# A decoder block on one Trainium2 core: a third merge-gate pair in the block scheme, fewer score matmuls for compressed keys, half buffers for attention weights

## The chip, the core and the metric

The kernel runs on one core of a Trainium2 chip. The core has a matmul engine (PE, with its weight loads PEld), a vector engine (DVE), an activation engine (ACT), a general engine (POOL) and a queue engine (SP) that issues most transfers; POOL issues some too. The engines run their own instruction lists in order and wait for each other through semaphores. PE writes to PSUM, eight banks of 128 x 512 float32; all else lies in SBUF or in the memory of the chip.

The metric is the time of one execution on the device in microseconds. Three runs of the kernel before took 1549.4, 1545.86 and 1548.6 us; their median is 1548.6.

## The reference

One layer of a hybrid decoder block, batch 1, 1024 positions, width 1024, all in float32. What is computed, cut to its core:

```python
h = rms_norm(x, norm1_g)
zq, zkv, zg, zr, zm = split(h @ w_in)              # 512, 768, 24, 2048, 2048 columns
y_nsa = nsa_attention(zq, zkv, zg, ...)            # 8 heads of 64 in 2 groups, 3 branches
y_ret = retention(zr)                              # 4 heads of 128
u = stack([y_nsa @ w_branch[0], y_ret @ w_branch[1]])
gates = sigmoid(zm)                                # 2 x 1024 columns: the merge gates
x = x + sum(gates * u) @ w_out
h = rms_norm(x, norm2_g)
x = x + (silu(h @ ffn_w_gate) * (h @ ffn_w_up)) @ ffn_w_down      # 2816 wide
```

The attention has three branches with one softmax each: compressed keys (63 blocks, from a small network over overlapping blocks of 32 positions), eight selected blocks of 64 keys (chosen by the compressed branch's weights), and a window of 512 keys. Scores are q.k/8 minus a slope per head times the distance, and masked:

```python
sc = einsum('btgrd,bngd->bgrtn', qg, kc) * scale - slopes * c_dist
p_cmp = masked_softmax(sc, c_dist >= 0)
```

## The kernel before

**Numbers.** A float32 product is made of three fast products: each operand is split into a high and a low part (ACT copies the high part, DVE subtracts to get the low one; a "fill"), and hi.hi, hi.lo and lo.hi are accumulated in one PSUM bank. So one product of 128 output rows, 512 columns and a depth of 512 is 12 matmuls with 512 moving columns.

**Block scheme.** Large products are done as 2 x 2 blocks with seven block products in place of eight (Strassen-Winograd); sums of blocks are made on DVE. For the input projection the scheme runs over pairs of 128-column units (`r_pairs`, L474): `gseq` (L1139) lists the block products as (product, pair), `g_loads` (L1154) fetches the two weight tiles of each pair, `g_ops` and `g_wsums` make operands, `g_main` issues the matmuls, `g_store` and the functions beside it add up and store the results. Before the change the pairs are two of merge gates (columns 7 and 6 of `m_units`) and eight of retention. The first two pairs do all seven products here; for the retention pairs, products 1 and 2 are done earlier by `gates_first` (L912) and fetched back from memory.

**Merge gates done directly.** The other six columns of merge gates, 12 units of 128 columns, are done by `merge_gates` (L1533) with `half_mm`: two halves of 24 matmuls for each unit. They have the lowest priority in the attention stage, so the scheduler puts them wherever PE has nothing else to do. In the rows these are matmuls from H, the normalised input, against `wh`.

**Attention.** 16 units `u` = (group, block of 128 queries); `us` lists them. For each, `cmp_all` (L1569) does the compressed branch: eight matmuls write four heads' scores, for each head one with the high part of the compressed keys (`kc[:, g, 0]`) and one with the low part; then DVE's `ttr` adds the mask table `Mc`, scales and finds the maximum in one instruction; ACT takes the exponential. `produce_all` (L1644) does the scores of the two other branches in blocks of two heads, into buffers P of two rows of 1024; `p_exp` and `p_scale` turn them into weights; `consume_all` (L1706) transposes them on PE four tiles at a time into a PSUM bank psT, splits them into pT (ACT, then DVE) and multiplies them with the values into psO. Query tiles `qt` come from memory through POOL into two buffers (`q_loads`); a buffer is free again when the scores that use it are done (`q_drop`). `P_ring` has three P buffers, given out in turn.

**Retention** shares the stage with attention. When the last unit's output y is stored, `y_loads` fetches it back, and the branch projections, the output projection and the FFN follow.

**The order.** The work is written as generators that yield operations. `Sched` (L161) keeps a time for each engine and each tile by a table of costs and always issues the operation that could start first; ties go by priority. `SLACK` (L50) is how much earlier than needed an operand has to be ready before an operation counts as startable: 600 ns for PE. Each cost has a duration and a latency until others see the result. All this happens when the program is built; on the chip the order is fixed.

## Time and profile before

| what | value |
|---|---|
| median of three runs | 1548.6 us |
| profiled execution | 1546.82 us |
| its span, first to last instruction | 1545.1 us |
| mean granted clock of PE | 0.997 |
| 0 to 120 us: PE busy | 115.37 us |
| 120 to 330 us (projections): PE busy | 209.12 us |
| 330 to 780 us (attention, retention, merge gates): PE busy | 442.08 us |
| 780 to 930 us (merge, output projection): PE busy | 148.56 us |
| 930 to 1320 us (FFN up): PE busy | 389.65 us |
| 1320 us to the end (FFN down): PE busy | 219.63 us |

In the rows of the profile, `out<-in` are the program's tile names; psS, psT, psO and psF are groups of PSUM banks (three, two, one and two). `xN` counts the instructions of a row. In a timeline row the first number is the start in us, the second the time to the last end of the group; consecutive matmuls overlap, so the time that one costs is read from start to start. A bracket gives the idle time of the engine before the row and what ended it. PE busy times include matmuls' overlapping ends.

### The profile page before, as it was taken

What the parts mean: (1) busy time and instruction counts of PE and PEld (TensorE: products, weight loads), DVE (VectorE), ACT (ScalarE), POOL (GpSimd) and SP (SyncE); (2) the same over time, 40 slices, a digit from 0 to 9 for tenths busy, and PEclk for the clock granted to TensorE, in tenths of its full rate; (3) what the DMA queues carried; (4) which work ended last, traced back from release to release, by engine and by line L of the source; (5) the groups of instructions that cost most, each with busy time, mean ns of one, the idle gap of its engine ahead of it and who ended that gap; (6) DMA issues with size and microseconds to landing.
All of it is one profiled execution on the core that took longest, in us unless ns stands there. A gap on an engine that the chain in (4) does not pass through costs nothing.

```text
span 1545.1 us, 22782 instructions
## 1 busy us (share of the span) xinstructions
PE 1524.4 (99%) x7959; PEld 1300.2 (84%) x7959; DVE 1111.2 (72%) x2364; ACT 754.7 (49%) x1527; POOL 262.5 (17%) x367
## 2 busy tenths in 40 slices
PE   9999999999999999999999999999999999999998
PEld 8887888888899988888888887888888888888887
DVE  7677967738798867798667467777667767676674
ACT  6355542218767777777415335433334333444442
POOL 3001400012232221221000001232332333000000
PEclk9999999999999999999999999999999999999999
DMA  7975975463432444244493224244544544597421
GB/s 219 257 236 168 299 233 161 144 201 92 141 104 78 126 132 130 83 142 153 150 341 129 104 82 123 96 136 141 186 140 145 184 145 144 201 381 255 163 69 55
DMA packets 210421, 249.79 MB, mean 162 GB/s; under 512 B 22657, under 2 KB 138369, under 8 KB 209410
## 3 DMA queue, kind: packets, MB, share of 16 engines
q1 hardware_dynamic: 197186, 206.39, 41.4%
q0 software_dynamic: 13120, 41.95, 8.7%
q8 instruction: 62, 1.02, 0.3%
q14 instruction: 53, 0.43, 0.1%
HBM read 171.73 MB, written 78.66 MB: 162 GB/s over the span
## 4 chain that ended last, share of the span: by engine, by line
PE 88%; DVE 6%; DMA 2%; ACT 1%; issue 1%; POOL 1%; SPq 1%; DVEq 0%; POOLq 0%; ACTq 0%
PE psS L316 31%; PE psF L316 27%; PE psO L316 14%; PE psT L316 11%; PE psT L321 5%; DVE P L1567 1%; DMA qt<-q_scr 1%; DMA yraw<-y_scr 1%; PE psF L321 1%; SPq L370 1%; PE psO L321 1%; DVE pT L346 0%; DVE H L346 0%; DVE P L351 0%; ACT P L336 0%
## 5 line engine op out<-in xcount | busy, mean ns | idle before, releaser
L316 PE MATMUL psF<-H,wh 128*128 128x512 f32 x876 | 223.9, 394 | 0.0
L316 PEld LDWEIGHTS psF<-H,wh 128*128 128x128 f32 x876 | 160.5, 188 | 29.3 <-ACT aw L336 0.4
L316 PE MATMUL psS<-H,wh 128*128 128x512 f32 (+1 forms) x678 | 167.0, 378 | 0.5 <-ACT H L336 0.5
L316 PEld LDWEIGHTS psS<-H,wh 128*128 128x128 f32 x678 | 115.9, 189 | 18.3 <-ACT H L336 1.0
L336 ACT ACTIVATE P<-P,pm 128x640 f32<-128x640 f32 (+7 forms) x128 | 94.1, 736 | 45.4 <-DVE pm L1567 43.5
L346 DVE TENSOR_TENSOR pT<-psT,pT 128x512 fp32r<-128x512 f32 (+1 forms) x152 | 91.6, 615 | 27.9 <-ACT pT L336 27.6
L316 PE MATMUL psS<-kT,qt 128*128 128x384 f32 (+3 forms) x384 | 102.3, 346 | 0.0
L316 PE MATMUL psO<-pT,vv 128*128 128x256 f32 x528 | 92.0, 291 | 2.5 <-DVE pT L346 2.5
L336 ACT ACTIVATE pT<-psT 128x512 fp32r<-128x512 f32 (+1 forms) x152 | 77.2, 534 | 34.2 <-PE psT L321 33.6
L316 PEld LDWEIGHTS psO<-pT,vv 128*128 128x128 f32 x528 | 78.7, 189 | 11.0 <-DVE pT L346 4.8
L321 PE MATMUL psT<-ident,P 128*128 128x128 f32 x528 | 76.9, 273 | 0.7 <-DVE pT L346 0.6
L346 DVE TENSOR_TENSOR wh<-wraw,wh 128x512 fp32r<-128x512 f32 (+1 forms) x66 | 60.0, 913 | 20.2 <-ACT wh L336 20.1
L336 ACT ACTIVATE wh<-wraw 128x512 fp32r<-128x512 f32 (+1 forms) x67 | 53.6, 805 | 42.2 <-PE psT L316 17.8
L316 PEld LDWEIGHTS psS<-kT,qt 128*128 128x128 f32 x384 | 63.9, 190 | 6.5 <-DVE pm L1567 0.8
L321 PEld LDWEIGHTS psT<-ident,P 128*128 128x128 f32 x528 | 61.2, 140 | 4.8 <-issue 1.2
L316 PE MATMUL psS<-wo,H 128*128 128x512 f32 x216 | 58.6, 392 | 0.0
L336 ACT ACTIVATE P<-P,pc 128x640 f32<-128x640 f32 (+7 forms) x68 | 46.9, 710 | 11.9 <-DVE pc L346 11.4
L316 PE MATMUL psS<-op 128*128 128x512 f32 (+1 forms) x240 | 51.1, 354 | 0.0
L369 POOL DMA_DIRECT2D qt<-q_scr x16 | 12.2, 764 | 218.9 <-PE psF L316 130.9
L316 PE MATMUL psF<-sh,op 128*128 128x512 f32 x192 | 46.7, 391 | 0.8 <-DVE sh L346 0.6
L316 PEld LDWEIGHTS psS<-wo,H 128*128 128x128 f32 x216 | 40.2, 188 | 8.1
L316 PEld LDWEIGHTS psS<-op 128*128 128x128 f32 x240 | 41.0, 189 | 6.9
(588 smaller groups left out, 3628.7 us busy)
## 6 DMA issues: line engine op xcount, KB each, us to landing
wraw<-in_w_in_dram SPq DMA_DIRECT2D x30, 512.0 KB, 4.3
f_scr<-fs SPq DMA_DIRECT2D x22, 512.0 KB, 3.6
row<-in_ffn_w_down_dram POOLq DMA_DIRECT2D x22, 512.0 KB, 4.6
t_scr<-row POOLq DMA_DIRECT2D x22, 512.0 KB, 3.6
qt<-q_scr POOLq DMA_DIRECT2D x16, 512.0 KB, 4.5
st<-t_scr SPq DMA_DIRECT2D x31, 256.0 KB, 4.2
z_scr<-zs SPq DMA_DIRECT2D x24, 256.0 KB, 2.0
wraw<-in_ffn_w_gate_dram SPq DMA_DIRECT2D x12, 512.0 KB, 3.9
```

Source lines behind the costliest of these rows:

```text
L316: lambda: pe.matmul(o, l, r, start=start, stop=stop, skip_group_check=True))
L321: return Op("pe", 109, 100, [o], [i], lambda: pe.transpose(o, i, ident))
L336: return Op("act", c, 150, outs, ins, lambda: act.activation(o, i, func, scale=scale, **kw))
L346: return vop(o, [a, b], lambda: (eng or dve).tensor_tensor(o, a, b, op), eng)
L369: r = Op("gp", 1040, lat, [o], [i], lambda: gp.dma_start(o, i)) if eng is gp else \
L370: Op("sp", 50, lat, [o], [i], lambda: sp.dma_start(o, i))
L1567: lambda: dve.tensor_tensor_reduce(o, a, b, -sc, init, ALU.add, ALU.min, acc))
```

## The change

- `NZ = 3`: the first three pairs of the block scheme are merge gates (columns 7, 6 and 5). The third pair's products are listed in a sequence of its own in `gseq`, and the places that distinguished pairs 0 and 1 from the others compare with NZ. `merge_gates` does columns 4 to 0: 10 units.
- Compressed scores: the mask table `Mc` becomes an operand of PE (fp32r, made in Mw's space and copied). For each unit one matmul with the identity writes the mask to the first 64 of each head's 128 columns; then one matmul a head multiplies the queries with both parts of the keys at once, 128 columns: the high part's scores are added to the mask, the low part's scores stand beside them. ACT copies the low part's scores to the new tile cB, and `ttr` adds it in the place where it added the mask.
- P buffers: a block of up to 512 keys takes a half buffer. `Parts` gives out six halves by a plan made ahead (`P_plan`); larger blocks take two halves of one buffer.
- The scheduler's table: PE's slack 240 ns in place of 600, the latency of a matmul's result 230 in place of 100, the costs of matmuls and of POOL's operations set anew.

```diff
-SLACK = {"pe": 600.0, "act": 40.0, "dve": 40.0, "gp": 0.0, "sp": 0.0}
+SLACK = {"pe": 240.0, "act": 40.0, "dve": 40.0, "gp": 0.0, "sp": 0.0}
...
+class Parts(Ring):
+
+
+    def __init__(self, tiles, plan):
+        self.tiles, self.plan, self.n, self.busy, self.was = tiles, plan, 0, {}, {}
+
+    def units(self):
+        a, w = self.plan[self.n]
+        return range(a, a + w)
+
+    def can(self):
+        return not any(u in self.busy for u in self.units())
+
+    def alloc(self, sched):
+        us = self.units()
+        t = self.tiles[us[0] // 2][:, :, us[0] % 2 * 512:us[0] % 2 * 512 + 512 * len(us)]
...
-        c = max(108.0, n * RATE[0] + 3) if r.dtype == F32R else 4 * max(53.5, n * 0.4167 + 1)
-        return Op("pe", c, 100, [o], [l, r],
+        c = max(111.0, n * 0.4427 + 5 if n < 512 else 227.0) if r.dtype == F32R else 4 * max(53.5, n * 0.4167 + 1)
+        return Op("pe", c, 230, [o], [l, r],
...
-            return Op("gp", 70 + 2.4 * n, 150, [o], ins, fn)
+            return Op("gp", 180 + 2.3 * n, 70, [o], ins, fn)
...
-    r_pairs = [(-1, 7), (-1, 6)] + [(h, i) for h in range(4) for i in (2, 0)]
+    NZ = 3
+    r_pairs = [(-1, 7 - n) for n in range(NZ)] + [(h, i) for h in range(4) for i in (2, 0)]
...
     for f in range(2, GN):
-        gseq += [(6, f), (4, f - 1), (5, f), (3, f - 1), (7, f)]
+        if f < NZ:
+            gseq += [(1, f), (4, f - 1), (2, f), (3, f - 1), (6, f), (5, f), (7, f)]
+        else:
+            gseq += [(6, f), (4, f - 1), (5, f), (3, f - 1), (7, f)]
...
-        for c in range(5, -1, -1):
+        for c in range(7 - NZ, -1, -1):
...
-    P_ring = sb_ring(ap_, [128, 2, T], F32, "P", 3)
+    P_plan, at = [], 0
+    for (g_, i_), br_, pr_ in blocks:
+        w = 2 if i_ >= 4 else 1
+        at += at % 2 if w == 2 else 0
+        P_plan.append((at % 6, w))
+        at += w
+    P_ring = Parts([ap_.tile([128, 2, T], F32, name="P", bufs=3) for _ in range(3)], P_plan)
...
+            sv = s.rearrange("p (r a n) -> p r a n", r=4, a=2)
+            yield mm(sv[:, :, 0, :], identr, Mc[:, None, 56 - 8 * i:120 - 8 * i].to_broadcast([128, 4, 64]), True, False)
             for r in range(4):
-                yield mm(s[:, r * 64:(r + 1) * 64], qt[u][:, 0, r, :], kc[:, g, 0, :], True, False)
-                yield mm(s[:, r * 64:(r + 1) * 64], qt[u][:, 0, r, :], kc[:, g, 1, :], False, True)
+                yield mm(s[:, r * 128:(r + 1) * 128], qt[u][:, 0, r, :], kc[:, g].rearrange("p a n -> p (a n)"), False, r == 3)
             q_drop(u)
+            sB = fresh(ap_, [128, 4, 64], F32, "cB")
+            yield ac(sB, sv[:, :, 1, :])
             for r in range(4):
-                yield ttr(P[:, r, :], s[:, r * 64:(r + 1) * 64], Mc[:, 56 - 8 * i:120 - 8 * i],
-                          2.0 ** -(4 * g + r + 1), 3e38, m[:, r:r + 1])
+                yield ttr(P[:, r, :], sv[:, r, 0, :], sB[:, r, :], 2.0 ** -(4 * g + r + 1), 3e38, m[:, r:r + 1])
```

Over the whole program PE has 7805 instructions before and 7743 after: 12 fewer of 512 columns, 128 matmuls of 64 columns replaced by 64 of 128 and 16 of 256, two fewer of the matmuls that warm PE up at the start. ACT has 16 copies more. The order of all engines is made anew; from the end of the output projection on it is the same on PE but for a few matmuls that change places by one.

What stands on PE in the projection stage, before. The rows are block products of 12 matmuls each, named by their operands (gRS, gSa, gSb and H are blocks of the input and their sums; wh and oq hold weights):

```order
L316 MATMUL psF<-gSb,oq 128x512 x12
L316 MATMUL psS<-gRS,oq 128x512 x12
L316 MATMUL psS<-gRS,wh 128x512 x12
L316 MATMUL psS<-H,wh 128x512 x12
L316 MATMUL psO<-gSa,wh 128x512 x12
L316 MATMUL psF<-gSb,wh 128x512 x12
L316 MATMUL psS<-gRS,oq 128x512 x24
```

The same place on PE after:

```order
L346 MATMUL psF<-gSb,oq 128x512 x12
L346 MATMUL psS<-gRS,oq 128x512 x12
L346 MATMUL psS<-H,wh 128x512 x24
L346 MATMUL psT<-H,wh 128x512 x12
L346 MATMUL psF<-gSb,wh 128x512 x12
L346 MATMUL psS<-gRS,oq 128x512 x12
L346 MATMUL psO<-gSa,oq 128x512 x12
L346 MATMUL psS<-gRS,oq 128x512 x24
```

The third pair's products 1 and 2 (the rows from H into psS and psT) have come in between the second pair's last ones, and its products 6, 5 and 7 follow.

What stands on PE ahead of the compressed scores of the third unit of the second group, before. With buffer numbers: qt_5810 is the query tile of the unit before, qt_6132 the one that is waited for; kT0 and kT1 are keys, kc the compressed keys; rd, re, rS and rc belong to retention. The last use of the tile whose buffer qt_6132 takes stands six rows above the first row shown:

```order
L316 MATMUL psO_6099<-pT_6112,vv1_5863 128x256 x2
L321 MATMUL psT_6148<-ident_78,P_5939 128x128 x2
L316 MATMUL psS_6155<-kT1_5635,qt_5810 128x256 x2
L316 MATMUL psF_6091<-rd_5577,re_6088 128x128
L316 MATMUL psF_6091<-rS_5801,rc_6047 128x128
L316 MATMUL psF_6091<-rd_5577,re_6088 128x128
L316 MATMUL psS_5817<-H_85,wh_5075 128x512 x2
L316 MATMUL psO_6099<-pT_6151,vv1_5863 128x256 x2
L321 MATMUL psT_6187<-ident_78,P_6042 128x128 x2
L316 MATMUL psS_6145<-kc_146,qt_6132 128x64 x8
```

The same place on PE after (qt_5822 is the tile of the unit before, qt_6084 the new one); the last use of the buffer's old tile stands nine rows above the first row shown:

```order
L346 MATMUL psF_6053<-rd_5744,re_6049 128x128
L346 MATMUL psF_6053<-rS_5911,rc_5913 128x128
L346 MATMUL psS_6124<-kT1_5653,qt_5822 128x256 x2
L346 MATMUL psF_6053<-rd_5744,re_6049 128x128
L346 MATMUL psO_6117<-pcT_5692,vc_150 128x512
L351 MATMUL psT_6134<-ident_78,P_3144 128x128 x2
L346 MATMUL psS_6144<-kT0_5821,qt_5822 128x256 x2
L351 MATMUL psT_6136<-ident_78,cPd_5987 128x128 x4
L346 MATMUL psS_5761<-H_85,wh_4924 128x512 x5
L346 MATMUL psS_6174<-kT0_5821,qt_5822 128x256 x2
L346 MATMUL psS_6186<-Mc_154,identr_83 128x4x64
L346 MATMUL psS_6186<-kc_149,qt_6084 128x128 x4
```

More of the unit's own scores (rows with kT0, kT1 and qt_5822) now stand ahead of the next unit's compressed scores, which are a mask matmul and four of 128 columns where there were eight of 64.

What stands on PE at the end of attention, before (psO<-pT,vv are output products, psT<-ident,P transpositions of weights):

```order
L316 MATMUL psF<-H,wh 128x512 x5
L316 MATMUL psO<-pT,vv_6095 128x256 x4
L316 MATMUL psF<-H,wh 128x512 x3
L316 MATMUL psO<-pT,vv_6095 128x256 x4
L316 MATMUL psF<-H,wh 128x512 x45
L316 MATMUL psS<-H,wh 128x512 x36
```

And after:

```order
L346 MATMUL psF<-H,wh 128x512 x5
L346 MATMUL psO<-pT,vv_6102 128x256 x4
L346 MATMUL psF<-H,wh 128x512 x3
L346 MATMUL psO<-pT,vv_6102 128x256 x4
L346 MATMUL psF<-H,wh 128x512 x42
L346 MATMUL psS<-H,wh 128x512 x36
```

Three matmuls fewer stand between the last output product and the first that needs its result (in the psS row).

More of the change, by code (lines that the diff above doesn't have):

```diff
@@ L137, in release @@
         raise ValueError("not live")
+class Parts(Ring):
[9 more added lines that the diff above has]
+        t = self.tiles[us[0] // 2][:, :, us[0] % 2 * 512:us[0] % 2 * 512 + 512 * len(us)]
+        name = key(t)[0]
+        for u in us:
+            for hh in range(2):
+                k = (name, hh * 2 + u % 2)
+                sched.seed[k] = sched.used.get(k, 0.0)
+            self.busy[u] = t
+        self.n += 1
+        return t
+    def release(self, t):
+        for u in [u for u, e in self.busy.items() if e is t]:
+            del self.busy[u]
 class Bag(Ring):
@@ L319, in tr @@
         if i.dtype == F32R:
-            return Op("pe", 56, 100, [o], [i], lambda: pe.transpose(o.bitcast(F32R), i, identr))
-        return Op("pe", 109, 100, [o], [i], lambda: pe.transpose(o, i, ident))
+            return Op("pe", 56, 230, [o], [i], lambda: pe.transpose(o.bitcast(F32R), i, identr))
+        return Op("pe", 109, 230, [o], [i], lambda: pe.transpose(o, i, ident))
     def ac(o, i, scale=1.0, func=AF.Copy, bias=None, accum=None):
@@ L401 @@
         "H": lambda off: off // 1024 % NT,
-        "P": lambda off: off // 1024,
+        "P": lambda off: off // 512,
         "xx": lambda off: off // 1024,
@@ L480 @@
     GN = len(r_pairs)
-    z_units = [pair_unit(f, 0) for f in range(2, GN)]
+    z_units = [pair_unit(f, 0) for f in range(NZ, GN)]
     a_scr = [dram.tile([128, 512], F32, name=f"a_scr{f}") for f in range(GN)]
-    for c, b in ((7, 1), (7, 0), (6, 1), (6, 0)):
+    for c, b in [(7 - n, b) for n in range(NZ) for b in (1, 0)]:
         z_scr[c, b] = dram.tile([128, T], F32, name=f"z_scr{c}_{b}")
-    order = [u for c in range(5, -1, -1) for u in m_units[c][::-1]] + b_units[1] + b_units[0] + o_units[:4] + o_units[6:]
+    order = [u for c in range(7 - NZ, -1, -1) for u in m_units[c][::-1]] + b_units[1] + b_units[0] + o_units[:4] + o_units[6:]
     def half_mm(hl, half, o, k0=0, nk=8, mov=None, step=1):
@@ L504 @@
     gate = att.tile([128, NT, NH, 3], F32, name="gate")
-    Mc = att.tile([128, 128], F32, name="Mc")[:, 0:120]
+    Mc = att.tile([128, 128], F32R, name="Mc")[:, 0:120]
     few = att.tile([128, 8, 8], F32, name="few")
@@ L833, in tables @@
         fl.add("rt")
-        yield g(Mc, lambda: gp.iota(Mc, pattern=[[16, 120]], base=-865, channel_multiplier=-1, **kw))
-        yield sel(Mc, [[-16, 120]], NEG, 865, 1)
+        M0c = Mw[:, 0:120]
+        yield g(M0c, lambda: gp.iota(M0c, pattern=[[16, 120]], base=-865, channel_multiplier=-1, **kw))
+        yield sel(M0c, [[-16, 120]], NEG, 865, 1)
+        yield vcopy(Mc, M0c)
         yield g(valid0, lambda: gp.memset(valid0, 1.0))
@@ L913, in gates_first @@
         banks = {}
-        for f0 in range(2, GN, 2):
+        for f0 in range(NZ, GN, 2):
             for p, f in ((1, f0), (1, f0 + 1), (2, f0), (2, f0 + 1)):
-                u = z_units[f - 2]
+                u = z_units[f - NZ]
                 yield from unit(u)
@@ L1237, in g_wsums @@
         g_drop(f)
-        yield Wait(lambda: ("g6", f) in fl and (f > 1 or (2, f) in gops))
+        yield Wait(lambda: ("g6", f) in fl and (f >= NZ or (2, f) in gops))
         yield tt(b, G[:, 4:8], b, ALU.subtract)
@@ L1282, in g_main @@
             elif p == 6:
-                if f > 1:
+                if f >= NZ:
                     Y[f] = yield Alloc(gy_ring)
                     sch.spawn(g_a_load(f), 1)
-                yield Wait(lambda: f > 1 or ("gy1", f) in fl)
-                yield from g_prod(6, f, Y[f], f > 1, False)
+                yield Wait(lambda: f >= NZ or ("gy1", f) in fl)
+                yield from g_prod(6, f, Y[f], f >= NZ, False)
                 sch.spawn(g_y6(f, Y[f]), 1)
@@ L1306, in g_store @@
         if src is not None:
-            if f > 1:
+            if f >= NZ:
                 yield tt(t, src, gt["a", f], ALU.add)
@@ L1344, in g_y6 @@
         u = gt["u", f] = yield Alloc(gm["aw"])
-        yield tt(u, Y, gt["a", f], ALU.add) if f > 1 else ac(u, Y)
+        yield tt(u, Y, gt["a", f], ALU.add) if f >= NZ else ac(u, Y)
         fl.add(("gy6", f))
@@ L1349, in g_y7 @@
         W = yield Alloc(gm["aw"])
-        yield tt(W, Y, gt["a", f], ALU.add) if f > 1 else ac(W, Y)
+        yield tt(W, Y, gt["a", f], ALU.add) if f >= NZ else ac(W, Y)
         fl.add(("gy7", f))
```

## The prediction

> **What bounds the kernel now.** I read the page's busy times first, then the stages, then what PE (the matmul engine) waits for.
>
> ```profile
> span 1545.1 us, 22782 instructions
> PE 1524.4 (99%) x7959; PEld 1300.2 (84%) x7959; DVE 1111.2 (72%) x2364; ACT 754.7 (49%) x1527; POOL 262.5 (17%) x367
> ```
>
> PE is busy for all but 20.7 us of the span. So a matmul that goes is worth its own time, unless a wait takes its place. By stage (columns: length, then busy time and instruction count of PE, weight loads, DVE, ACT, POOL):
>
> ```profile
> 120.00:330.00 210.00, 209.12 (x938) 172.38 (x937) 153.44 (x267) 86.03 (x152) 27.09 (x23) 0.99 0.64 192
> 330.00:780.00 450.00, 442.08 (x2812) 394.30 (x2811) 346.86 (x1129) 307.74 (x735) 95.57 (x169) 1.00 0.42 128
> 930.00:1320.00 390.00, 389.65 (x1891) 328.67 (x1891) 280.50 (x432) 157.68 (x280) 116.10 (x116) 1.00 0.44 146
> ```
>
> The projections before 330 us and the FFN from 930 us have nothing to gain but work: PE idles 0.9 and 0.4 us there. Attention, 330 to 780 us, has 7.9 us of idle, and it is where DVE is loaded. The waits of PE over the whole span:
>
> ```profile
> PE psS L316 <- DMA qt<-q_scr: 2.8, 2, 1.6
> PE psO L316 <- DVE pT L346: 2.5, 6, 0.8
> PE psS L316 <- DVE pm L1567: 0.9, 1, 0.9
> ```
>
> The columns are sum, times, longest. The longest waits of attention are for a query tile on its way from memory (qt). Next comes the transposed attention weight (pT) that DVE finishes.
>
> **Work removed.** The unit of price is the first row here, of the chain of waits:
>
> ```profile
> 206.28 2.72 PE psS L316 x12
> 766.17 10.38 PE L316 MATMUL psF<-H,wh 128*128 128x512 f32 x45
> ```
>
> Twelve matmuls with 512 moving columns take 2.72 us, 0.227 each; the second row, of the timeline, gives the same with H as the moving operand. A merge pair done directly is 2 x 2 x 24 = 96 of them; in the block scheme it is 7 products x 12 = 84. That is 12 fewer: **-2.7 us**. The 84 stand in the projection stage (+19.0 us there), the 96 leave attention, where they were filler.
>
> The scores of the compressed keys, for one of the 16 units, in time order (start, duration to the last end, count):
>
> ```profile
> 544.63 1.08 PE L316 MATMUL psS<-kc,qt 128*128 128x64 f32 x8 [1.28 <-DMA qt<-q_scr]
> 545.54 1.17 PE L316 MATMUL psS<-H,wh 128*128 128x512 f32 x4
> ```
>
> Eight matmuls of 64 columns take 0.91 us from start to start of the next kind, 0.114 each. After the change there are four of 128 columns and one of 256 (the mask through the identity). The nearest rows for four of 128, and for 256:
>
> ```profile
> 347.34 0.56 PE L316 MATMUL psS<-kT,qt 128*128 128x128 f32 x4
> 347.74 0.62 PE L321 MATMUL psT<-ident,cPd 128*128 128x128 f32 x4
> 348.11 0.69 PE L316 MATMUL psS<-kT,qt 128*128 128x128 f32 x4
> 348.64 0.62 PE L321 MATMUL psF<-ident,rb 128*128 128x128 f32 x4
> 1318.11 0.88 PE L316 MATMUL psS<-H,wh 128*128 128x256 f32 x6
> 1318.83 2.91 PE L316 MATMUL psT<-H,wh 128*128 128x512 f32 x12
> ```
>
> Four take 0.40 to 0.53 us, and six of 256 columns 0.72, 0.12 each. I take 0.44 + 0.12 = 0.56, so a unit saves 0.35 us and sixteen **-5.6 us** (ends: 0.52 and 0.65 a unit, -6.2 and -4.2). So 128 columns cost no more than 64: the saving is in the count.
>
> A matmul with a repeated moving operand, whose output lies in four runs of 64 columns, is in no row. As four matmuls of 64 it would be 0.46 us instead of 0.12, 5.4 us more over sixteen; below 0.12 nothing brings it, since it moves 256 columns. I take 0.12: the 45 matmuls above read their moving operand H in four runs of 128, too, and go at the full 0.227.
>
> The Trainium skill speaks against this part. Its page "PSUM — Partial Sum Buffer", section "Specifications (TRN2)", says that a non-contiguous access pattern in PSUM slows matmuls significantly, and the mask's output is one. By it the 0.12 would be too low; no row of this case has such an output, and the page gives no figure.
>
> **Work added beside PE.** ACT copies half of the scores bank to SBUF for each unit (128x256), and DVE then adds it where it added the mask:
>
> ```profile
> 742.67 0.39 ACT L336 ACTIVATE pT<-psT 128x256 fp32r<-128x256 f32 x1 [1.39 <-PE psT L321]
> 340.00:740.00 400.00, 392.61 (x2550) 352.27 (x2549) 322.89 (x1088) 292.61 (x712) 92.68 (x163) 1.00 0.40 120
> ```
>
> 16 x 0.39 = 6.2 us on ACT, which is busy 73% in attention: nothing on the path. But it holds one of the two score banks 0.4 us longer, and the next score matmuls queue behind it on PE; that is in the price of the thinner distances below. DVE's count stays (64 additions of 64 columns, as before).
>
> The third pair needs two weight loads of 512 KB earlier on SP, and its operands on ACT and DVE: seven fills, four sums and some four outputs.
>
> ```profile
> 320.55 0.69 DVE L346 TENSOR_TENSOR gt<-psS,gt 128x512 f32<-128x512 f32 x1 [2.03 <-PE psS L316]
> ```
>
> Fifteen such DVE operations are 10.4 us, and DVE is at 153.44 of 210 us in that stage; PE gets 19.0 us more to hide them, and the stores are as many as before. I take nothing for it; if its first operand came late, the nearest row is 0.9 us, all the idle of that stage.
>
> **Query tiles.** The new order leaves more PE work between the last use of a query tile and the first of the tile that takes its buffer:
>
> ```profile
> L369 POOL DMA_DIRECT2D qt<-q_scr x16: 733/762/796, 323.5 to 674.8; - x16
> DMA to landing us min/median/max: 4.0/4.5/10.3
> 567.62 1.08 PE L316 MATMUL psS<-kc,qt 128*128 128x64 f32 x8 [1.56 <-DMA qt<-q_scr]
> ```
>
> A reload takes 0.76 + 4.5 = 5.3 us. Counted through the order at the durations above, the two that waited had 3.4 and 5.5 us of PE work; now they have 5.9 and 12.9, since half buffers for P let the small units' scores stand earlier. The shortest of the fourteen is now 4.8; eight between 4.9 and 5.5 stood before, seven of them without a wait. I count both waits as gone: **-2.8 us**; ends 0 and -2.8.
>
> **Distances in attention.** 719 filler matmuls (H against weights) stood between the first compressed score and the last output product; now 627. PE has 92 x 0.227 + 5.6 = 26.5 us less there, DVE has the same work. By the row of 340 to 740 us DVE goes from 322.89 of 400 (81%) to 322.89 of 373.5 (86%). What that does is shown by two stretches:
>
> ```profile
> 420.00:460.00 40.00, 40.00 (x280) 36.95 (x279) 34.97 (x132) 26.95 (x65) 13.73 (x26) 1.00 0.27 83
> 660.00:700.00 40.00, 38.67 (x229) 33.95 (x228) 37.40 (x102) 31.15 (x66) 8.53 (x15) 1.00 0.55 169
> ```
>
> At 87% of DVE PE idles nothing, at 94% 1.3 us of 40. So the mean is bearable, the peaks are not free. The trip that counts goes from a transposition through ACT and DVE to the product:
>
> ```profile
> 751.24 1.04 PE L321 MATMUL psT<-ident,P 128*128 128x128 f32 x8
> 751.88 1.09 ACT L336 ACTIVATE pT<-psT 128x512 fp32r<-128x512 f32 x2 [1.14 <-PE psT L321]
> 752.51 1.29 DVE L346 TENSOR_TENSOR pT<-psT,pT 128x512 fp32r<-128x512 f32 x2 [1.42 <-ACT pT L336]
> 753.96 0.64 PE L316 MATMUL psO<-pT,vv 128*128 128x256 f32 x4
> ```
>
> Over the 152 banks, the PE work put between them falls from a median 2.7 us to 2.5, and banks with under 2.0 rise from 22 to 37. A wait of this kind is 2.5 / 6 = 0.42 us. Fifteen more are 6.3 us at most, 0 at least. I take half, **+3.1 us**: a wait of PE also lets DVE catch up.
>
> **Ends of attention and the output projection.** After the last output product y goes through memory and back, covered by filler:
>
> ```profile
> 779.12 3.07 PE L316 MATMUL psS<-H,wh 128*128 128x512 f32 x11 [0.54 <-ACT H L336]
> 861.86 1.06 PE L321 MATMUL psT<-ident,hx 128*128 128x128 f32 x8 [0.30 <-DVE hx L356]
> ```
>
> PE waits 0.54 us there even with the 45 matmuls quoted above in between; the new order has 42: 3 x 0.227, **+0.7 us** (0 to 0.7). In the output projection the first transpositions of hx move up by four matmuls, 0.9 us, and one at 861.86 waits already: **+0.4**, half of it (0 to 0.9). From there on PE's order is the same but for a few matmuls that change places by one.
>
> Sum: -2.7 - 5.6 - 2.8 + 3.1 + 0.7 + 0.4 = **-6.9 us**. The profiled execution took 1546.8 us, 1.7 over its span, and the median of the runs is 1.8 above it. So 1539.9 for an execution like the profiled one, and 1548.6 - 6.9 = **1541.7** as a median.
>
> **Rivals.**
> - *DVE becomes the bound of attention* (slower). If the uneven load of DVE does not let the stage shrink by more than half of 26.5 us, 13.2 us come back as idle in place of my 3.1 - 2.8 = 0.3: 1541.7 + 12.9 = 1554.6. For it: the stretch at 94%, and thinner distances everywhere. Against: 87% without idle, and the new mean is 86%. It decides from some 10 us of new idle in attention, where the sum turns to a loss. Chance 0.10.
> - *The stage gets smoother.* Half buffers fill P further ahead, and the waits named above (2.8, 2.5, 0.9) go without new ones: -8.3 - 6.2 + 1.1 = -13.4, 1535.2. For it: the gaps of the query tiles. Against: the shorter trips. Chance 0.17.
> - *The mask matmul is slow, or the scores save nothing.* At 0.46 us the -5.6 becomes -0.2: 1547.1. For it only that no row shows such an output; against it the 0.227 of the split reads. The PSUM page's rule named above would lead here. Chance 0.10.
> - The forecast, with its neighbours: 0.63.
>
> **Range and chances.** The two ends of my terms give -6.2 - 2.7 - 2.8 = -11.7 without new waits, and -4.2 - 2.7 + 6.3 + 0.7 + 0.9 + 0.9 = +1.9 with all of them: 1536.9 to 1550.5. The smoother case lies just below, the mask's inside, so 1535 to 1550 leaves out the DVE case and some tails. Faster by over 0.2% (3.1 us, about what a measurement of this kernel can tell from no change): most of the forecast, 0.52, and the smoother case, 0.17: 0.69. Within 0.2%: 0.10 of the mask, 0.08 of the forecast and 0.01 of the DVE case. Slower: 0.09 and 0.03.
>
> **What would show it.** Right: 84 more matmuls before attention without idle there; compressed scores at 0.56 us a unit; no wait of psS for qt near the group change; DVE near 86% in attention; PE's idle there about 8 us. The mask step is wrong if its matmul takes over 0.2 us to the next start, the query step if psS still waits for qt. The forecast is wrong if idle in attention is above 15 us or below 3.

## The result, and the profile after

The changed kernel took **1562.4 us** (median of 4 runs, 1560.07 to 1563.35) where the kernel before took 1548.15 on the same chip: a ratio of 1.0085, 95% interval 1.0071 to 1.0100. It is slower, by about 13 us; the forecast was 7 us faster. A second set of six runs gave 1561.29 and 1.0079 (e5 below).

The page of the changed kernel, with the profiled execution at 1561.77 us:

```profile
span 1560.1 us, 22719 instructions
PE 1528.0 (98%) x7897; PEld 1297.4 (83%) x7897; DVE 1123.2 (72%) x2383; ACT 757.1 (49%) x1544; POOL 273.6 (18%) x368
```

PE has 62 matmuls fewer in the records and is busy longer, 1528.0 us for 1524.4; its idle rose from 20.7 to 32.1 us. So part of the loss is idle, and part is matmuls that took longer. Both stand in a table by stage. The first fence is the kernel before, the second the changed one, cut at the same places of the program: the first compressed score, the last product of attention weights with values, the first matmul with the output weight, the end of that projection, and the end. The columns are the stretch, its length, then busy time and count of PE, weight loads, DVE, ACT and POOL, PE's granted clock, the DMA share and GB/s.

```profile
0.00:341.40 341.40, 335.89 (x1661) 283.17 (x1662) 242.65 (x426) 144.14 (x257) 44.86 (x71) 0.99 0.71 213
341.40:766.10 424.70, 417.31 (x2704) 374.39 (x2703) 339.98 (x1119) 304.21 (x730) 92.68 (x163) 1.00 0.39 121
815.60:909.70 94.10, 93.58 (x440) 77.39 (x439) 53.56 (x88) 37.02 (x78) 6.63 (x14) 1.00 0.33 112
```

```profile
0.00:365.10 365.10, 355.53 (x1743) 297.29 (x1744) 253.11 (x441) 150.95 (x271) 51.11 (x71) 1.00 0.68 202
365.10:776.10 411.00, 399.97 (x2562) 356.61 (x2561) 341.46 (x1124) 299.73 (x734) 90.25 (x163) 0.98 0.40 123
824.80:925.30 100.50, 95.75 (x440) 78.45 (x439) 52.09 (x86) 36.73 (x76) 14.02 (x15) 0.98 0.30 105
```

To part work from waiting I went through PE's matmuls from start to start and took off what each form takes when nothing is waited for (512 columns 0.227 us, 256 columns 0.12, 128 columns 0.11, the other forms likewise). The first part is called *work* here, what is left *over*: waits and matmuls at a lower clock.

| stage | before us | after us | difference | of it work | of it over |
|---|---|---|---|---|---|
| to the first compressed score | 341.4 | 365.1 | +23.7 | +18.7 | +5.0 |
| attention | 424.7 | 411.0 | -13.7 | -26.4 | +12.7 |
| branch matmuls behind it | 49.5 | 48.7 | -0.8 | -0.7 | -0.1 |
| output projection | 94.1 | 100.5 | +6.4 | 0 | +6.4 |
| the rest | 635.4 | 634.8 | -0.6 | 0 | -0.6 |
| sum | 1545.1 | 1560.1 | +15.0 | -8.4 | +23.4 |

**The work fell by 8.4 us, as the prediction has it (2.7 + 5.6 = 8.3). The over grew by 23.4 us**, in three stages, for which the prediction had 0, 0.3 (3.1 - 2.8) and 0.4. Some 7 us of it are clock: leaving out the first 30 us and the last, the trace has PE's granted clock at 0.5 for 17.1 us (10.24 from 374.35 us, 3.41 each from 691.79 and 835.15), the kernel before for 3.41, and by estimate half of the difference is lost time. The waits of PE after the change (sum, times, longest):

```profile
PE psT L351 <- DVE hx L386: 3.0, 2, 1.5
PE psS L346 <- POOL wo L376: 2.8, 1, 2.8
PE psF L346 <- DVE wh L376: 2.6, 2, 2.1
PE psO L346 <- DVE pT L376: 1.9, 5, 0.9
PE psT L351 <- DVE pcT L376: 1.8, 1, 1.8
PE psS L346 <- DVE pm L1609: 1.6, 2, 1.1
PE psS L346 <- ACT cP L366: 1.5, 1, 1.5
PE psS L346 <- DMA qt<-q_scr: 0.9, 1, 0.9
```

The wait for pT, which the prediction feared, fell from 2.5 to 1.9 us, and that for qt from 2.8 to 0.9. What came are single events that were not there before. The two largest, on the timeline (start, duration, engine, instruction, count; in brackets the idle before it and what ended it; rows in between are left out):

```profile
365.11 0.56 PE L346 MATMUL psS<-kc,qt 128*128 128x128 f32 x4
370.76 0.38 ACT L366 ACTIVATE cB<-psS 128x256 f32<-128x256 f32 x1 [5.54 <-DMA r_scr<-ga]
370.82 0.55 POOL L1545 IOTA Mt<- 128x512 f32 x1 [14.16 <-DMA r_scr<-ga]
371.99 0.41 PE L346 MATMUL psS<-kT,qt 128*128 128x128 f32 x2 [1.49 <-ACT cP L366]
373.81 0.44 PE L346 MATMUL psS<-kT,qt 128*128 128x128 f32 x2 [1.13 <-DVE pm L1609]
374.82 1.11 PE L351 MATMUL psT<-ident,cPd 128*128 128x128 f32 x4 [0.58 <-POOL cPd L376]
382.48 1.63 PE L346 MATMUL psS<-H,wh 128*128 128x512 f32 x3
...
826.26 7.42 POOL L376 TENSOR_TENSOR wo<-wor,wo 128x1024 fp32r<-128x1024 f32 x1 [91.69 <-DVE sgx L386]
833.74 6.46 PE L346 MATMUL psS<-wo,H 128*128 128x512 f32 x20 [2.85 <-POOL wo L376]
```

The same two places in the kernel before:

```profile
341.43 0.97 PE L316 MATMUL psS<-kc,qt 128*128 128x64 f32 x8
342.65 0.22 DVE L1567 CUSTOM_DVE_ANT_0 cP<-psS,Mc 128x64 f32<-128x64 f32 x1 [6.68 <-DMA qt<-q_scr]
...
818.94 1.22 DVE L346 TENSOR_TENSOR wo<-wor,wo 128x1024 fp32r<-128x1024 f32 x1
```

At the start of attention the scores of the first unit are there at 365.7 us, but ACT's copy of them waits until 370.76 for the store of a retention result (ga, to r_scr) to reach memory: cB is the first tile written in a pool (ap) that lies on the space of the buffers ga. PE then waits in three places in a row, and its matmuls go slowly for 10 us: four transpositions take 1.11 us instead of 0.62. In the output projection one weight split stands on POOL, where it takes 7.42 us; before the change all of these splits stood on DVE, at 1.2 us each. A third event, a wait of 1.84 us until 690.49 us, also begins with a weight split on POOL; its rows stand in the last section.

### The profile page after: what moved, and what is told of

The parts are those of the page before. It is cut to its first block, busy times and chain, and to the rows that moved or that the text cites. A ratio compares the mean times of both kernels' runs of the same rounds, so it can differ in the third digit from the quotient of the medians.

```text
span 1560.1 us, 22719 instructions
## 1 busy us (share of the span) xinstructions
PE 1528.0 (98%) x7897; PEld 1297.4 (83%) x7897; DVE 1123.2 (72%) x2383; ACT 757.1 (49%) x1544; POOL 273.6 (18%) x368
## 4 chain that ended last, share of the span: by engine, by line
PE 79%; DVE 9%; DMA 5%; ACT 3%; POOL 2%; issue 2%; SPq 1%; DVEq 0%; POOLq 0%; ACTq 0%
PE psS L346 26%; PE psF L346 24%; PE psO L346 13%; PE psT L346 11%; PE psT L351 4%; DVE P L1609 1%; DVE H L376 1%; DVE pT L376 1%; PE psF L351 1%; DMA r_scr<-ga 1%; ACT P L366 1%; SPq L400 1%; DVE P L381 1%; PE psO L351 0%; POOL wo L376 0%
## 5 line engine op out<-in xcount | busy, mean ns | idle before, releaser
L346 PE MATMUL psF<-H,wh 128*128 128x512 f32 x804 | 206.4, 396 | 1.4 <-ACT gR L366 0.8
L346 PEld LDWEIGHTS psF<-H,wh 128*128 128x128 f32 x804 | 147.7, 189 | 28.9 <-ACT gR L366 1.8
L346 PE MATMUL psS<-kT,qt 128*128 128x384 f32 (+3 forms) x384 | 105.6, 352 | 2.7 <-ACT cP L366 1.5
```

The costliest lines, as they stand in the source:

```text
L346: lambda: pe.matmul(o, l, r, start=start, stop=stop, skip_group_check=True))
```

## The experiments

Eighteen kernels. Times are medians; the ratio is to the kernel before on the same chip. Work and over are those of each run's one profiled execution, worked out as above, from PE's first matmul to its last (6 us less than the span). That execution can lie some us from the median: in e3 5 below, in e6 6 above, in e12 4 above.

| run | what it is | us | ratio, 95% interval | work | over |
|---|---|---|---|---|---|
| | before | 1548.2 | 1 | 1502.7 | 36.2 |
| | after | 1562.4 | 1.0085 [1.0071, 1.0100] | 1494.3 | 59.6 |
| e1 | after, old planner numbers | 1562.7 | 1.0097 [1.0077, 1.0118] | 1494.5 | 59.2 |
| e2 | before, new planner numbers | 1560.1 | 1.0074 [1.0054, 1.0094] | 1502.5 | 49.5 |
| e3 | after, cP and cB apart | 1559.6 | 1.0076 [1.0054, 1.0097] | 1494.3 | 52.0 |
| e4 | after, weight split on DVE | 1555.9 | 1.0058 [1.0040, 1.0075] | 1494.3 | 57.0 |
| e5 | after, again | 1561.3 | 1.0079 [1.0063, 1.0095] | 1494.3 | 61.4 |
| e6 | after, new numbers in attention only | 1554.5 | 1.0043 [1.0025, 1.0060] | 1494.5 | 58.3 |
| e7 | after, two pairs | 1553.5 | 1.0032 [1.0019, 1.0045] | 1497.0 | 49.4 |
| e8 | after, old scores | 1562.2 | 1.0095 [1.0081, 1.0109] | 1499.7 | 54.4 |
| e9 | before + scores + half buffers | 1555.3 | 1.0045 [1.0033, 1.0057] | 1497.2 | 49.6 |
| e10 | before + third pair | 1565.0 | 1.0114 [1.0095, 1.0134] | 1500.0 | 57.2 |
| e11 | before + scores | 1551.7 | 1.0031 [1.0020, 1.0042] | 1497.2 | 46.6 |
| e12 | e7, new numbers in attention only | 1550.2 | 1.0012 [1.0001, 1.0023] | 1497.2 | 49.4 |
| e13 | e11, cover held back | 1557.4 | 1.0060 [1.0047, 1.0072] | 1497.2 | 52.2 |
| e14 | e1, cover held back | 1565.2 | 1.0111 [1.0097, 1.0126] | 1494.5 | 62.2 |
| e15 | before, slack 240 | 1577.2 | 1.0184 [1.0167, 1.0201] | 1502.5 | 67.1 |
| e16 | e7, new numbers from the merge gates to attention | 1552.2 | 1.0023 [1.0014, 1.0031] | 1497.2 | 47.1 |
| e17 | after, slack 600 | 1571.4 | 1.0149 [1.0132, 1.0166] | 1494.6 | 70.5 |
| e18 | e3 and e4 together | 1553.0 | 1.0041 [1.0027, 1.0056] | 1494.3 | 50.6 |

Read down the last two columns: every edit takes off the work that was forecast for it (the pair 2.7, the scores 5.5), and every kernel but the one before has at least 10 us more over in its profile (by the ratios at least 7, in e12). **No version beats the kernel before**; e12 comes nearest.

### The planner's numbers against the edits of the work (e1, e2, e15, e17)

e1 puts all four of the planner's numbers back in the changed kernel, e2 puts the new ones into the kernel before. e15 and e17 move the slack alone:

```diff
-SLACK = {"pe": 240.0, ...
+SLACK = {"pe": 600.0, ...            (e1, e17; e2 and e15 the other way)
-        return Op("pe", c, 230, [o], [l, r],
+        return Op("pe", c, 100, [o], [l, r],          (e1; e2 the other way)
-            return Op("gp", 180 + 2.3 * n, 70, [o], ins, fn)
+            return Op("gp", 70 + 2.4 * n, 150, [o], ins, fn)   (e1; e2 the other way)
```

> The changed kernel with the planner's numbers of before: PE's slack 600 instead of 240, a latency of 100 instead of 230 behind a matmul, the old matmul and POOL costs. The third pair, the new scores and the half buffers stay. Theory A (the new numbers make a tighter order, and its stalls are the loss; the three edits of the work are worth the sum of the prediction): about 1542 us, 20 below the changed kernel, with idle of PE in the head and in the output projection as before. Theory B (the three edits themselves lose, the third pair by taking filler out of attention): within 3 us of the changed kernel, 1559 to 1565. Theory C (the first unit of attention waits for a store that lands late, whatever the numbers): 1550 to 1556, and the copy of cB on ACT still waits some 5 us for r_scr.

> The kernel before with the planner's numbers of the changed kernel, nothing else. Theory A: slower than before by what the change lost plus what its edits were worth, 14 + 7 = 21 us, 1569 us; at least 10 slower. Theory B and theory C: within 3 us of the kernel before, 1545 to 1551.

Measured: 1.0097 and 1.0074. Each half of the change by itself loses about as much as the whole; theory A (the numbers are the loss) falls with e1, theory B (the edits are) with e2. Theory C (the store is late whatever the numbers) falls with e1, too: its copy of cB starts at 361.95 us, 0.7 behind the first score, after a wait of 0.83 for qt. In e1 the head is as in the kernel before: its first compressed score starts at 361.2 us, 3.9 earlier than after the change. In e2 it starts at 345.6, 4.2 later than before. So the new numbers cost the head 4 us, with or without the third pair. What e1 loses lies elsewhere, in a wait of 7.59 us right behind attention. The timeline of e1, and its row of PE's waits:

```profile
779.37 0.63 PE L346 MATMUL psO<-pT,vv 128*128 128x256 f32 x3 [0.18 <-DVE pT L376]
779.84 1.52 PE L346 MATMUL psS<-H,wh 128*128 128x512 f32 x6
788.95 1.65 PE L346 MATMUL psS<-H,wh 128*128 128x512 f32 x3 [7.59 <-ACT H L366]
...
PE psS L346 <- ACT H L366: 8.4, 2, 7.6
```

The output of attention goes through memory and back there. Before, 45 branch matmuls (psF) covered that trip; e1 has none left. With the old slack the planner has used them up inside attention.

> The kernel before with PE's slack 240 instead of 600, the other numbers as before. If the slack is what e2 lost by (1560): 1556 to 1561, with the waits of the head (93 us, 58 us, 21 us) in it. If the latency, matmul and POOL costs are: 1547 to 1550, and the head as before.

> The changed kernel with one number put back: PE's slack 600 instead of 240; latency, matmul and POOL costs stay new. Theory S (the slack of 240 is by itself what the change lost by): the waits of the head and of the output projection go, 11 us, 1550 to 1552. Theory K (the slack moves idle from one place to another: with 600 the branch matmuls are used up inside attention and none stand behind it, as in e1): the head as in the kernel before, but a wait of over 5 us with half-speed matmuls behind attention, 1559 to 1565.

Measured: 1.0184 and 1.0149, worse than any theory had it. The planner counts a chain from PE through another engine back to PE with the latency of the matmul plus PE's slack: 700 ns in the kernel before and in e1, 470 after the change, 340 in e15, 830 in e17. With the work of before, 470 costs 11 us (e2, where the cost formulas changed, too) and 340 costs 28 (e15): PE waits more in all stages up to the output projection (over in e15 against before: head +7.5, attention +13.9, behind it +8.3). That chains are planned tighter than they run is the likely reason; no run shows it by itself. With the work of after, 830 costs 11 us more than 470 (e17 against e5): the cover behind attention is used up. e17's rows show it as e1's do:

```profile
PE psS L346 <- ACT H L366: 8.4, 2, 7.5
792.02 1.54 PE L346 MATMUL psS<-H,wh 128*128 128x512 f32 x6
```

So theory K holds for the end of attention: with 600 and the third pair no cover is left (e1, e10 and e17 have none), with 240 there are 42 matmuls. It fails for the head, which was to be as before: e17's first compressed score starts at 366.7 us, where the changed kernel has 365.1 and e5 368.1. The head loses with the slack of 240 alone (e15, 348.4 for 341.4 us) and with the other new numbers alone (e17); so its loss is not simply the price of the cover.

### The two named waits (e3, e4, e18; e5 as a control)

```diff
+    apc = es.enter_context(tc.tile_pool(name="apc", bufs=1))          (e3, e18)
     kvp = es.enter_context(tc.tile_pool(name="kvp", bufs=1))
-            P = fresh(ap_, [128, 4, 64], F32, "cP")
+            P = fresh(apc, [128, 4, 64], F32, "cP")
-            sB = fresh(ap_, [128, 4, 64], F32, "cB")
+            sB = fresh(apc, [128, 4, 64], F32, "cB")
...
-        yield Any(tt(*lo), tt(*lo, gp))
+        yield tt(*lo)                                   (in wo_split: e4, e18)
```

> The changed kernel with cP and cB in a small pool of their own, opened ahead of the others, so that they lie where the first-stage weights lay and not in a pool that lies on the buffers ga. PE's order is the same. Theory C: the copy of cB starts within 1 us of its scores instead of 5.5 us behind them, the waits of PE at 370 to 376 us of the profile go with the half-speed matmuls behind them, and of the 10.9 us over nominal that I count for 350 to 400 us some 7 to 9 go: 1553 to 1555 us. Theories A and B: 1560 to 1564, since the copy is only the first of several waits there.

> The changed kernel with the split of the output weight that the planner put on POOL (7.42 us in the profile) kept on DVE, as in the kernel before. If that split is a cause by itself: the wait of 2.85 us at 831 us goes, and some 10 matmuls behind it take 0.23 instead of 0.43 us: 5 us less, 1557. If another engine is late there anyway: 1561 to 1563.

> The changed kernel once more, unchanged, as a control on the same chip as the next three: both theories 1559 to 1565. Its own runs so far had clocks between 0.99 and 1.00, and e3 ran from 1554 to 1565 with clocks from 0.999 down to 0.992; if the spread is the clock, here too the slow runs show the low clock.

> e3 and e4 together: the changed kernel with cP and cB in a pool of their own and the late weight split on DVE. If the two named waits are losses by themselves, their worths add: by the medians (2 and 6 us) 1554 us, by the profiles of e3 and after (8 us less over nominal in attention, 4 less in the output projection) 1549 to 1550. If one mend only uncovers the next wait: 1556 to 1560.

e3 did to its place what theory C says. Its copy, and the stretch that held the wait, in e3 and then in the changed kernel:

```profile
366.16 0.38 ACT L366 ACTIVATE cB<-psS 128x256 f32<-128x256 f32 x1 [0.53 <-DMA qt<-q_scr]
350.00:400.00 50.00, 47.31 (x272) 40.24 (x271) 34.33 (x145) 31.86 (x104) 15.11 (x45) 1.00 0.67 198
```

```profile
350.00:400.00 50.00, 45.77 (x234) 38.72 (x233) 28.89 (x125) 26.86 (x90) 12.39 (x41) 0.90 0.67 185
```

The copy no longer waits for the store, the granted clock of the stretch is 1.00 instead of 0.90, and 38 matmuls more are in it. The over of attention fell by 8.1 us in that profile, 5.5 of them in the first 20 us of the stage; it is the fastest of the six executions. The six, though, went from 1554 to 1565, and the interval of e3 overlaps that of e5: by itself the mend is not separated by time. e4 took 1555.9, 5 us under e5, with intervals that overlap as well; in its profile the split takes 1.22 us on DVE and the wait is 0.79 us. Together (e18) they are separated: 1.0041 [1.0027, 1.0056] against 1.0079 [1.0063, 1.0095] of e5 on another chip, 5.9 us by the ratios, near the sum of 1554 that was expected from the medians. So the two events are real losses of some 6 us, a little under half of the 12 to 13.

Where the rest stands, e18's profile shows. Against the kernel before it has 14.4 us more over: 4.2 in the head, 4.3 in the first 20 us of attention (a wait of 1.13 us for cPd is left there), 3.9 in the 45 us around the wait of 1.84 us that follows a weight split on POOL, 1.8 behind the branch matmuls. With 8.4 us less work that makes 6.0 us, and the ratio says 6.3. No run takes out the wait of 1.84 us by itself, so its worth is read from the trace alone.

### Each edit undone or alone (e7 to e11)

e7 and e10 set NZ to 2 in the changed kernel, and to 3 in the kernel before; the other three take the new scores and the half buffers out or bring them in, line for line as the diff of the change has them.

> The changed kernel with two pairs instead of three, its new scores, half buffers and planner's numbers kept. Theory F (the third pair takes filler that attention needs, and its 12 saved matmuls are worth less): faster than the changed kernel by 4 to 8 us, 1554 to 1558, with less idle of PE in attention. Theory G (filler is not short under the new numbers, and the waits come from single chains): slower by the 12 matmuls, 1563 to 1566.

> The changed kernel with the compressed scores of before: eight matmuls of 64 columns a unit, the mask on DVE, no copy on ACT. If the prediction's term stands (0.35 us of PE a unit, 16 units): 5.6 us slower, 1567 to 1568. If the time saved there only went into PE's waits: 1561 to 1563. If the copy on ACT is what makes the start of attention wait: faster, 1553 to 1556.

> The kernel before with the new scores and the half buffers only: two pairs, and the planner's numbers of before. Theory F (the two edits inside attention keep their worth as long as filler is thick there; the loss is the third pair and the planner's numbers): the prediction's scores term, 1548 - 5.6 = 1542 to 1543 us. Theory H (the time saved on PE turns into waits for DVE with any filler): 1546 to 1549.

> The kernel before with the third pair only: scores, buffers and planner's numbers of before. Theory F: the waits of attention that e1 showed come back, 10 to 20 us slower than before, 1558 to 1568, with a wait of several us just behind attention. The prediction's term for the pair by itself (12 matmuls fewer, thinner cover 3 us): 1548 to 1549.

> The kernel before with the new scores only. Theory F: 1542 to 1543 us, as e9 without the half buffers; if the half buffers are worth anything e9 is below this one. Theory H: 1546 to 1549.

e7: 1.0032, separated from e5; **the third pair costs 7 us where it saves 2.7 of work**. e10 agrees: alone it costs 18 us. That is theory F for the pair. e8: 1.0095, 2.5 us above e5 by the ratios and not separated from it, so whether the 5.4 us of work that the new scores take off are in the time of the changed kernel is not settled. The copy on ACT is not what makes the start wait: without it, DVE's first instruction there waits for the same store until 369.71 us. e9 and e11 missed every expectation: the scores alone make the kernel before *slower* by 4.8 us, with the half buffers by 7.0 (the two are not separated). The timeline of e11 shows where (SP's issues left out between):

```profile
770.65 1.99 PE L346 MATMUL psF<-H,wh 128*128 128x512 f32 x8
770.85 0.60 ACT L366 ACTIVATE y<-psO 128x512 f32<-128x512 f32 x1 [2.21 <-PE psO L346]
772.48 1.52 PE L346 MATMUL psS<-H,wh 128*128 128x512 f32 x6
778.34 0.69 DVE L376 TENSOR_TENSOR yraw<-yraw 128x512 f32<-128x512 f32 x1 [8.97 <-DMA yraw<-y_scr]
779.06 0.63 ACT L366 ACTIVATE H<-yraw 128x512 fp32r<-128x512 f32 x1 [7.62 <-DVE yraw L376]
779.74 1.65 PE L346 MATMUL psS<-H,wh 128*128 128x512 f32 x3 [5.75 <-ACT H L366]
```

Eight branch matmuls stand behind the last product, where the kernel before has 45. The scores saved 5.5 us of PE inside attention; the planner gave that time to 37 branch matmuls from behind it (8.4 us), attention got 5.3 us longer, not shorter, and the trip through memory lay bare. Where the edits are counted against a kernel with cover to spare, they do earn: from e2 to e7 (the new numbers, two pairs in both) scores and half buffers together bring 6.5 us by the ratios, 5.6 of it forecast.

### The numbers by stage (e6, e12, e16)

```diff
+def costs(new):
+    NEW[0] = new
+    SLACK["pe"] = 240.0 if new else 600.0
...
     gls.close()
+    costs(True)          (e6, e12; e16 sets it where the merge gates start)
...
+    costs(False)
     lts.close()
```

> The changed kernel with the planner's new numbers for attention only; ahead of it and behind it the numbers of before. Theory A1 (the new numbers cost in the head and in the output projection, some 5 and 6 us of PE's waits and half-speed matmuls, and in attention they are needed, since e1 without them had 7.7 us of wait at its end): 1551 to 1553 us. Theory A2 (the three edits of the work cost as much under any numbers): 1560 or more.

> e7 with the planner's new numbers in attention only. Theory A1 (the new numbers cost some 6 us in the head and the output projection, whatever the pairs): 1547 to 1548. If they also help attention with two pairs: below e9. If the new numbers are harmless outside attention: 1553.

> e7 (two pairs, new scores, half buffers) with the planner's new numbers only from the merge gates of the head to the end of attention; ahead of them and behind them those of before. e7 has 17.8 us over nominal in its first 150 us, e9 9.4. Theory A1: 1553.5 - 8 = 1545 to 1546 us, a little faster than the kernel before. If what the head loses is made good by waiting later: 1551 to 1554.

Measured: 1.0043, 1.0012, 1.0023. Keeping the new numbers out of the head and the projection is worth some 6 us with three pairs (separated from e5), which speaks for A1; with two pairs e12 lies 3 us under e7, with intervals that overlap a little, and e16 is not separated from e7, and its 1552.2 us is the case in which the head's gain is made good by waiting later. Kept for attention, the new numbers do help: e12, with 144 branch matmuls left behind attention, lies 5 us under e9, which has the old numbers throughout and 8 left (same chip, intervals apart). The over of the first 150 us fell from 17.8 (e7) to 11.9 (e16), as expected, but 2.2 of that came back behind attention.

### The cover held back (e13, e14)

```diff
             for half in range(2):
+                if (c, half) >= (5, 1):
+                    yield Wait(lambda: "last" in fl)
                 sch.spawn(branch1_out(c, half), 3)
```

The flag is set when the last block of attention is consumed.

> e11 (the kernel before with the new scores only) with the last five groups of the branch matmuls held back until the last block of attention is consumed, so that 44 of them stand behind the last product with the values, as 45 did before, instead of 8. Theory F (the scores' gain is real and e11 lost it because the planner used the cover up early): the wait of 5.9 us at 774 us and the half-speed matmuls behind it go, 1551.7 - 9 = 1543 us. Theory H (attention is short of filler in any order): as much idle appears between the last blocks of attention, 1549 to 1552.

> e1 (all three edits with the planner's numbers of before) with the same five groups held back: 44 branch matmuls behind the last product with the values instead of none. Theory F: the wait of 7.7 us at 781 us with its half-speed matmuls goes, 1562.7 - 12 = 1551 us. Theory H: the idle moves ahead of the last block, 1559 or more.

Measured: 1.0060 and 1.0111, both slower than the kernels they start from (e14 not separated from e1). Theory F's 1543 and 1551 us are missed by 14; theory H's case fits e14 and is 5 us short for e13. In e13 there are 56 branch matmuls in one row behind the last product, and PE waits nonetheless:

```profile
735.00:765.50 30.50, 26.54 (x165) 21.95 (x165) 21.22 (x48) 18.83 (x33) 0.00 (x0) 1.00 0.11 35
765.59 13.08 PE L346 MATMUL psF<-H,wh 128*128 128x512 f32 x56
782.17 0.69 DVE L386 SCALAR_TENSOR_TENSOR sg<-sg,psF 128x512 f32<-128x512 f32 x1 [2.66 <-DMA sg<-z_scr]
782.91 1.50 PE L346 MATMUL psF<-H,wh 128*128 128x512 f32 x4 [4.24 <-DVE sg L386]
```

In the 30 us ahead PE idles 4.0 us for lack of filler (e11 has no idle in the same stretch), and behind, the branch sums need gates (sg) whose loads queue on SP behind the eight loads of y. A wait of 5.75 us for H became one of 4.24 for sg, and 4 us of idle ahead. In the over, e13 has 3.8 us less than e11 behind attention and 7.7 more in it, e14 6.7 less than e1 and 10.0 more. So what is shown is that this way of holding the cover back loses; since it also moves the gates' loads, another way is not excluded.

## Why the prediction was wrong

Its terms, one by one.

- **Work, -2.7 and -5.6: right.** 8.4 us of work went. A unit of compressed scores takes 0.52 us to the next start (forecast 0.56), and the mask's matmul 0.12, as taken; these rows of the changed kernel show both (start to start; 12 of the 16 mask matmuls go like this one, three that follow a matmul counted at 0.03 us have 0.20, and one at half clock 0.32):

```profile
420.91 0.28 PE L346 MATMUL psS<-Mc,identr 128*128 128x256 f32 x1
421.03 0.56 PE L346 MATMUL psS<-kc,qt 128*128 128x128 f32 x4
421.43 0.90 PE L346 MATMUL psS<-H,wh 128*128 128x512 f32 x3
```

  So the Trainium skill's sentence that any non-contiguous pattern slows matmuls significantly ("PSUM — Partial Sum Buffer", "Specifications (TRN2)") did not bear on four runs of 64 columns: 0.12 us is what six contiguous matmuls of 256 columns took each. The rival of a slow mask matmul was wrong; its other half, that the scores save nothing, is not settled in time (e8).
- **Query tiles, -2.8: nearly right.** 2.8 us became 0.9.
- **Distances, +3.1: the mechanism was wrong, and the size.** The waits for pT fell. Attention's over grew by 12.7 us through single chains: 7.5 of it in the first 20 us, where the first unit waited for the last retention store, and 4.2 in the 45 us around the wait of 1.84 us. The rival that DVE becomes the bound of attention gave 12.9 us for this stage; the amount is right by luck and the reason is not, since DVE is at 341.46 of 411 us there, 83%, below the 86% that the prediction held bearable. The prediction's own sign of being wrong, idle in attention above 15 us, did not show: PE idles 411.0 - 399.97 = 11.0 us there, 3.6 more than before. The greater part of the over is busy time, matmuls that took longer.
- **End of attention, +0.7: right for the changed kernel** (42 matmuls of cover, no loss). The experiments show how narrow that is: with 8 left the wait is 5.8 us, with none 7.6.
- **"I take nothing for it" (the third pair's operands): right for the operands, wrong for the stage.** With the old numbers the head of three pairs is 18.1 us longer than that of two (e10 against before; 21.2 for e1 against e9), for 19.0 us of matmuls. The stage lost 4 more by the planner's numbers, for which the sum had no term.
- **Output projection, +0.4: the term that was missed most plainly, +6.4 measured.** The prediction looked for what moves in PE's order, and found the transpositions of hx (their longest wait grew from 0.30 to 1.42 us). The new plan also moved one weight split from DVE to POOL, ahead of PE's next matmuls. POOL's rows have it in the changed kernel and not in the one before. With the split on DVE the stage takes 97.6 us (e4) or 96.6 (e18) for 100.5, so 3 to 4 of the 6.4 us are the split's. The new costs alone do not move it: in e2, e7 and e17, which have them, it stands on DVE.

What failed behind all of these is one step: **the prediction priced the removed work on PE and let the order stand.** In this kernel an edit of the work, or of the planner's numbers, gives a new order on all engines, and in this one the waits and slow matmuls grew by 23.4 us while 8.4 us of work went. The forecast's sign would have held only if the new order were as good as the old one, and no order tried here was. Not settled is whether such an order exists for the new work; e12, at 1.0012, comes near it. Also open is what share of the loss each part has, since the parts do not add: alone, the pair costs 18, the numbers 11 and the scores 5 us, and together 13.

## What to carry to other kernels

Work taken off a busy engine is time only if what it covered is covered still: count the matmuls that stand between the last product and the first use of its round trip, before and after, and price the trip without them. Where a planner makes the order, compare the order on every engine, and look at each instruction that changed its engine; "the same on PE" is not the same. And expect a good order to lose something with any edit: 7 us of over or more, by the ratios, came with each one here, so a gain on paper should be larger than that, or the order be tuned again with it.

## What the runs showed of the hardware

**A short wait can slow the matmuls behind it.** In the changed kernel PE waited 1.84 us until 690.49 us and 2.85 us until 833.74. Behind each wait, 1.3 and 1.4 us later, the granted clock fell to 0.5 for 3.41 us, and the matmuls went slowly: those of 512 columns took 0.427 us from start to start instead of 0.227. The slow ones add 1.6 us to the first wait and 1.7 to the second. The Trainium skill ("TensorE: Matmul & The Clock Gate", "Part 1: The HAM clock gate") has the clock halve after an idle window of about 3.4 us; here less idle than that was enough. It was not enough each time: in e5, the same kernel, PE waited the same 1.84 us until 690.87 us, and the clock stayed at 1.0 behind it. The time of a run goes with the clock: over 74 runs of the kernel before, those with a mean granted clock of 0.998 had a median of 1546.4 us, those with 0.995 one of 1551.1. So how much a wait costs differs from run to run.

**DVE and POOL slow each other.** The split of 128x1024 took 2.56 us on POOL at 686.6 us, and DVE's operation of that moment took 2.87 us, where the same operation takes 0.68:

```profile
681.81 0.68 DVE L376 TENSOR_TENSOR H<-yraw,H 128x512 fp32r<-128x512 f32 x1
686.60 2.56 POOL L376 TENSOR_TENSOR wh<-wraw,wh 128x1024 fp32r<-128x1024 f32 x1 [7.67 <-ACT wh L366]
686.84 2.87 DVE L376 TENSOR_TENSOR H<-yraw,H 128x512 fp32r<-128x512 f32 x1
690.49 0.44 PE L351 MATMUL psT<-ident,P 128*128 128x128 f32 x2 [1.84 <-DVE pcT L376]
```

At 826 us it was the other way round: DVE's operations, one behind the other until 831.49 us, kept their times, and POOL's took 7.42 us; it ended 2.2 us behind the last of them. The Trainium skill ("SBUF — State Buffer", "SBUF: two separate sides") calls the two engines' shared port pair an exclusive lock whose loser fully blocks, and both rows agree with it: when DVE's operation began, POOL's had 2.32 us to go, and with DVE's own 0.68 that makes 3.0 for the 2.87. In e8 the same split of wo, begun on POOL 0.22 us ahead of a DVE split, took 2.41 us, and the DVE split 3.27 for its 1.22. A planner that may choose between the two needs a price for the neighbour, not only for itself.
